# A decoder layer on one NeuronCore: the local-attention branch product as seven quarter products, GpSimd's additions on VectorE, and tables that fix places and orders

## The chip, the cores and the metric

The kernel runs on one core of one Trainium2 chip. The metric is the device time of one execution in microseconds (us); lower is better. A core has TensorE (PE in the profile; its weight loads are PEld), VectorE (DVE), ScalarE (ACT), GpSimd (POOL) and SyncE (SP), which here only issues transfers. Each engine works through its own instructions in a fixed order; semaphores make one wait for another. All arithmetic that decides the time is in float32, with TensorE reading a rounded format (`fp32r`).

## The reference, cut to what matters

One layer on x of 512 tokens by 1024, with three token mixers side by side, gates, an output projection and a gated feed-forward block:

```python
u = rms_norm(h, ln_mix_pre[l])
proj = jnp.einsum('bsd,de->bse', u, w_in[l])
qa, ka, va, qb, kb, vb, qm, gl = jnp.split(proj, split_idx, axis=-1)
y_swa = swa_sink_attention(...)         # local attention, 8 heads of 64, window 128
y_sb = stick_breaking_attention(...)    # 8 heads of 64
mkv = jnp.einsum('bmd,de->bme', rms_norm(mem, ln_mem[l]), w_mem_kv[l])
y_mem = memory_cross_attention(...)     # 4 heads of 128 on 256 memory rows
g = jax.nn.sigmoid(gl.reshape(B, S, N_BRANCH, D))
merged = (g[:, :, 0] * jnp.einsum('bse,ed->bsd', y_swa, w_branch_swa[l])
          + g[:, :, 1] * jnp.einsum('bse,ed->bsd', y_sb, w_branch_sb[l])
          + g[:, :, 2] * jnp.einsum('bse,ed->bsd', y_mem, w_branch_mem[l]))
mix = jnp.einsum('bsd,de->bse', merged, w_out[l])
h = h + rms_norm(mix, ln_mix_post[l])
u = rms_norm(h, ln_ffn_pre[l])
a = jax.nn.silu(jnp.einsum('bsd,df->bsf', u, w_gate[l])) * jnp.einsum('bsd,df->bsf', u, w_up[l])
h = h + rms_norm(jnp.einsum('bsf,fd->bsd', a, w_down[l]), ln_ffn_post[l])
```

The part that changes is `einsum(y_swa, w_branch_swa)`: 512 tokens by 512, times 512 by 1024.

## The kernel before, in words

**Three matmuls for one product.** Each operand x is split into a high part, x rounded to `fp32r` on ScalarE (line 137), and a low part, x minus the high part, on VectorE (line 138). A product is then three matmuls (`mm3`, lines 169 to 171): high by high, high by low, low by high.

**The stream of weights.** Weights come in pieces of 128 x 1024 (512 KB). `Stream` (line 34) holds a list of units. Each has a load (up to four units ahead), a split (up to three units ahead) and a generator of matmuls that yields its estimated time after each small group. `dn.run(us)` lets the stream issue that much work; between such calls the program issues the attention heads. So the code interleaves heavy products with attention, head by head. Four buffers each hold raw weights, high parts and low parts (`w_load`, `w_split`, lines 146 and 152).

**The order of the work.** The stream's units are, after the projections: the stick-breaking branch product, the gates of that branch, the gates of local attention, the product of local attention, the gates and the product of the memory branch. The memory heads (`mem_pair`, line 983) are issued in two pairs while the stream runs the local-attention product. One pair computes scores (`ms`), the softmax (`mw`: maxima, exponentials, scalings on line 1006), transposes (`mpt`, line 1012) and outputs (`ym`). The tile framework sorts what is issued into an order for each engine by its own estimates and by priorities; `after(...)` pins a few orders by hand.

**Seven products already in use.** The gates (`quart`, line 562) and the feed-forward block are computed with seven products of quarters in place of eight. Names p1 to p7 stand for these products. Their weights are sums of quarters, made by accumulating transfers on GpSimd's queue: `q_issue` (line 437) adds the next quarter from memory to a raw buffer that has been split (line 446). PSUM results are copied by ScalarE (line 540) or joined by VectorE.

**The branch product** (`branch_t`, line 577) is done plainly: for each half of the columns and each of four token tiles, four blocks of 128 by `mm3`, into one PSUM bank. VectorE multiplies the result by the gate (line 599). The addition to the sum of the branches (line 602) is GpSimd's, apart from the last token tile of the memory branch.

**Other work of GpSimd**: the sums of squares of the memory norm (lines 232 and 390), a low part of the position bias (line 810), scalings of the norms' gains (line 1058).

**Buffers.** 73 blocks of 128 x 512 (`ck`), 16 small ones, two PSUM pools of two and six banks (`dps`, `aps`). The weight pools are closed at the end of the mixers and their space is opened as the feed-forward's pool with nine raw buffers.

Of the kernel before, what the change touches and what calls it, by code (L numbers as in the profile page):

```python
# [29 lines left out]
QM_FIRST = 3  # L30
WARM = 10

# [74 lines left out]
def tile_kernel(ctx, tc, a):  # L107
    nc = tc.nc
# [4 lines left out]
    psd = ctx.enter_context(tc.tile_pool(name="psd", bufs=2, space=bass.MemoryType.PSUM))  # L113
    psa = ctx.enter_context(tc.tile_pool(name="psa", bufs=6, space=bass.MemoryType.PSUM))
    drm = ctx.enter_context(tc.tile_pool(name="drm", bufs=1, space=bass.MemoryType.DRAM))

    first = ExitStack()
    wp = first.enter_context(tc.tile_pool(name="wp", bufs=4))
    cst = first.enter_context(tc.tile_pool(name="cst", bufs=1))

    def ck(name, dt=F32):
        return ckp.tile([P, 512], dt, tag="ck", name=name)

    def small(name, n=4):
        return sm.tile([P, 8], F32, tag="s", name=name)[:, :n]

    def dps(name):
        return psd.tile([P, 512], F32, tag="d", name=name)

    def aps(name):  # L130
        return psa.tile([P, 512], F32, tag="a", name=name)
# [14 lines left out]
    def w_load(src, n):  # L146
        uid[0] += 1
        raw = wp.tile([P, 1024], F32, tag="raw", name=f"raw{uid[0]}")
        nc.sync.dma_start(raw[:, :n], src)
        return raw  # L150

    def w_split(raw, n):
        uid[0] += 1
        hi = wp.tile([P, 1024], F32R, tag="hi", name=f"hi{uid[0]}", bufs=4)
        lo = wp.tile([P, 1024], F32R, tag="lo", name=f"lo{uid[0]}", bufs=4)
# [32 lines left out]
    def after(ins, first):  # L188
        dep = mybir.DependencyInfo(mybir.DependencyClass.NoSync, mybir.DependencyReason.DATA)
        tc.add_manual_dep(ins.ins, first.ins.name, dep, reason="order")  # L190
# [18 lines left out]
    def const(name, shape, pool=cst):  # L209
        t = pool.tile(shape, F32, name=f"c_{name}")  # L210
        nc.sync.dma_start(t[:, :], a[name])
        return t
# [3 lines left out]
    ones = cst.tile([P, P], F32, name="ones")  # L216
# [11 lines left out]
    def rstd_of(name, acc, n, bank):  # L228


        if acc.shape[1] > n:
            nc.gpsimd.tensor_tensor(acc[:, :n], acc[:, :n], acc[:, n : 2 * n], op=ALU.add)
        ps = bank(f"ss_{name}")
        mm(ps[:, :n], ones[:, :], acc[:, :n], True, True)
        rb = cst.tile([P, n], F32, name=f"rb_{name}")
# [5 lines left out]
        rs = cst.tile([P, n // P], F32, name=f"rs_{name}")  # L241
# [102 lines left out]
    v_all = cst.tile([P, NT * 640], F32, name="v_all")  # L344
# [32 lines left out]
    def mem_split():  # L377
        acc = None
        for i, x in enumerate(st.pop("memT")):
# [9 lines left out]
            else:  # L389
                nc.gpsimd.tensor_tensor(acc[:, :], acc[:, :], x[:, :], op=ALU.add)  # L390
# [185 lines left out]

    def branch_t(b, h, q):


        def gen(hi, lo):  # L580
# [3 lines left out]
            for t in range(NT):  # L584
# [15 lines left out]
                eng = nc.vector if (b, t) == (MEM, NT - 1) else nc.gpsimd  # L600
# [27 lines left out]
    def add_proj(kind, idx, ci):  # L628
        dn.add(a["w_p"][:, ci].rearrange("p k n -> p (k n)"), 1024, proj(kind, idx))

# [24 lines left out]
    for b in (SB, SWA, MEM):  # L655
# [36 lines left out]
        if b != SB:  # L692
# [3 lines left out]
    xg = cst.tile([P, 544], F32, name="xg")  # L696
    g_pre, g_mem = xg[:, S : S + KC], xg[:, S + KC : S + 2 * KC]
    g_neg = cst.tile([P, KC], F32, name="g_neg")
# [20 lines left out]
    raws = [wp.tile([P, 1024], F32, tag="raw", name=f"raw_first{i}") for i in range(FIRST)]  # L719
    his = [wp.tile([P, 1024], F32R, tag="hi", name=f"hi_first{i}", bufs=4) for i in range(FIRST)]  # L720
    los = [wp.tile([P, 1024], F32R, tag="lo", name=f"lo_first{i}", bufs=4) for i in range(FIRST)]
# [10 lines left out]
    with tc.manual_schedule():  # L732

        idle = cst.tile([P, 512], BF16, name="idle")
# [48 lines left out]
    sinks = cst.tile([P, 8], F32, name="sinks")  # L783
# [3 lines left out]
    identb = cst.tile([P, P], BF16, name="identb")  # L787
    nc.gpsimd.tensor_copy(identb[:, :], ident[:, :])
    negm = cst.tile([P, P], BF16, name="negmb")
# [5 lines left out]
    def band_bias():  # L795
# [14 lines left out]
        nc.gpsimd.tensor_tensor(rbl[:32, :P], rb16[:32, :P], rbh[:32, :P].bitcast(F32), op=ALU.subtract)  # L810
# [25 lines left out]
    def pair_out(b, c, ps):  # L836

        y[(b, c)] = parts(f"y{b}{c}", ps)

# [293 lines left out]
    fac = {r: [(ck(f"{r}h{c}", F32R), ck(f"{r}l{c}", F32R)) for c in range(2)] for r in RIGHT}  # L1133
# [27 lines left out]
    def turn(t, tmp):  # L1161
# [5 lines left out]
        if t < 2:  # L1167
            turned[t] = [ck(f"ur{t}{h}") for h in range(2)]
            for h in range(2):
                place(("B11", "B21")[h], t, pt[h])  # L1170
                nc.scalar.copy(turned[t][h][:, :], pt[h][:, :])
# [4 lines left out]
        return place("T1", t, t1)  # L1176

# [21 lines left out]
    aq = {(i, j): [ck(f"aq{i}{j}{c}") for c in range(NCH)] for i in range(2) for j in range(2)}  # L1199
    sq = [ck(f"sq{c}") for c in range(NCH)]  # L1200
    sr = [ck(f"sr{c}") for c in range(NCH)]
# [16 lines left out]
    def g_raw(n, key, i, j):  # L1218
        uid[0] += 1
        gw[(n, key)] = fp.tile([P, 1024], F32, tag="raw", name=f"gw{uid[0]}")  # L1220
# [123 lines left out]
    ssd = [small(f"ssd{t}", 2) for t in range(NT)]  # L1344
# [8 lines left out]
    def dn_issue(p, c):  # L1353
# [3 lines left out]
        if p in ("p1", "p5", "p4"):  # L1357
            n = 512 * len(ks)
            src = a["w_dn"][:, h, j * HF + ks[0] : j * HF + ks[-1] + 1].rearrange("p k n -> p (k n)")
            if p == "p1":  # L1360
                rr[c] = fp.tile([P, 1024], F32, tag="raw", name=f"r{c}")
# [110 lines left out]
    first.close()  # L1472
    fp = ctx.enter_context(tc.tile_pool(name="fp", bufs=9, reuse_waits="tile"))

    def f_split(raw, n):
        uid[0] += 1
        hi = fp.tile([P, 1024], F32R, tag="hi", name=f"hi{uid[0]}", bufs=4)
        lo = fp.tile([P, 1024], F32R, tag="lo", name=f"lo{uid[0]}", bufs=4)
# [28 lines left out]
    load_at(4, g_raw, 0, "t", 1, 0)  # L1507
    load_at(4, g_plus, 0, "t", 0, 0)
# [34 lines left out]
    tmp[3] = mix(3)  # L1543
    turn(1, tmp[1])
    behind(since[-1], st["mixed"])
# [27 lines left out]
    go(len(fs.units))  # L1573

# [88 lines left out]
```

## Time and profile before

| | |
|---|---|
| runs | 787.07, 787.52, 788.17 us; median 787.52 |
| the profiled execution | 787.54 us |
| its span, first to last instruction | 785.7 us |
| granted TensorE clock, mean | 0.999 |
| PE busy | 776.3 us, 4638 matmuls |
| VectorE busy | 595.4 us |
| ScalarE busy | 469.3 us |
| GpSimd busy | 123.2 us |
| transfers | 128.61 MB |

The profile's times are counted from the start of the span; the device time is 1.84 us longer than the span. "PE busy" counts a matmul from its start to its modelled end, and consecutive matmuls overlap, so the distance from one start to the next tells the pace. "Idle before" is the time in which an engine did nothing ahead of an instruction, and the name behind the arrow is what ended it. The chain is followed back from the last instruction: at each step to what released it, or to the instruction before it on its engine.

### The profile page before, as it was taken

To read this page: it belongs to the slowest core of one execution; us is meant where nothing else is said; L and a number is where in the kernel's file an instruction comes from. 1 tells how busy PE (TensorE), PEld (TensorE's weight loads), DVE (VectorE), ACT (ScalarE), POOL (GpSimd) and SP (SyncE) were. 2 spreads that over 40 slices of the span, in tenths; PEclk is the share of its full clock that TensorE was granted. 3 is DMA by queue.
4 is the path that set the end of the run, shared out by engine and by line. 5 is a ranking of instruction groups with operands and counts; after the bars stand their busy time and mean duration, and the time that the engine had idled before them with its cause. 6 is when DMAs were issued, how large, how long until landed. Compare 5 with 4: busy or idle time off the path is not lost.

```text
span 785.7 us, 12335 instructions
## 1 busy us (share of the span) xinstructions
PE 776.3 (99%) x4638; PEld 682.2 (87%) x4638; DVE 595.4 (76%) x942; ACT 469.3 (60%) x837; POOL 123.2 (16%) x142
## 2 busy tenths in 40 slices
PE   9999999999999999999999999999999999999996
PEld 6899887788888888887888899999999999888885
DVE  6995876686877757876855599867677777898797
ACT  7663676686577666657633577455554455666673
POOL 0203400002011111321261000100000000215200
PEclk9999999999999999999999999999999999999999
DMA  8444923265449794369849418987666651949802
GB/s 301 132 138 121 314 88 108 81 190 124 89 100 206 178 208 139 54 170 250 304 162 255 92 47 219 260 220 191 186 180 183 186 155 54 222 107 239 184 1 108
DMA packets 44220, 128.61 MB, mean 164 GB/s; under 512 B 5248, under 2 KB 6832, under 8 KB 44160
## 3 DMA queue, kind: packets, MB, share of 16 engines
q1 hardware_dynamic: 30480, 85.21, 32.8%
q0 software_dynamic: 13248, 42.22, 27.8%
q8 instruction: 36, 0.59, 0.3%
q10 hardware_dynamic: 432, 0.39, 0.1%
q14 instruction: 24, 0.20, 0.1%
HBM read 120.98 MB, written 4.72 MB: 160 GB/s over the span
## 4 chain that ended last, share of the span: by engine, by line
PE 93%; DMA 2%; DVE 2%; issue 1%; ACT 1%; POOL 0%; DVEq 0%; SPq 0%; ACTq 0%; POOLq 0%
PE gx L169 5%; PE gx L171 5%; PE gx L170 5%; PE gy L171 3%; PE gy L169 3%; PE gy L170 3%; PE x L171 3%; PE x L170 3%; PE x L169 3%; PE br L169 2%; PE br L170 2%; PE br L171 2%; PE mx L171 2%; PE mx L170 2%; PE mx L169 2%; PE g1p L169 2%
## 5 line engine op out<-in xcount | busy, mean ns | idle before, releaser
L137 ACT CAST hi<-gw 128x1024 fp32r<-128x1024 f32 x77 | 79.9, 1048 | 92.7 <-DVE gw L1242 39.6
L138 DVE TENSOR_TENSOR lo<-raw,hi 128x1024 fp32r<-128x1024 f32 (+2 forms) x82 | 99.9, 1219 | 46.2 <-ACT hi L137 45.7
L138 DVE TENSOR_TENSOR lo<-gw,hi 128x1024 fp32r<-128x1024 f32 x77 | 93.5, 1223 | 36.2 <-ACT hi L137 36.2
L137 ACT CAST hi<-raw 128x1024 fp32r<-128x1024 f32 (+2 forms) x82 | 85.2, 1042 | 43.4 <-PE pv L171 13.0
L1224 POOL DMA_DIRECT2D gw<-in_w_gu x27 | 23.3, 883 | 196.4 <-DMA gw<-in_w_gu 91.3
L870 DVE TENSOR_TENSOR_SCAN bw<-br,bw 128x512 f32<-128x512 f32 (+3 forms) x32 | 24.4, 808 | 17.0 <-ACT bw L194 17.0
L137 ACT CAST hi<-r 128x1024 fp32r<-128x1024 f32 (+1 forms) x24 | 23.6, 982 | 19.8 <-PE y L171 5.3
L446 POOL DMA_DIRECT2D raw<-in_w_g x24 | 20.7, 862 | 93.2 <-DVE lo L138 74.2
L170 PE MATMUL x<-lo,lh 128*128 128x512 f32 x88 | 34.2, 389 | 0.0
L169 PE MATMUL x<-hi,lh 128*128 128x512 f32 x88 | 34.2, 389 | 0.0
L171 PE MATMUL x<-hi,ll 128*128 128x512 f32 x88 | 34.1, 389 | 0.0
L138 DVE TENSOR_TENSOR lo<-r,hi 128x1024 fp32r<-128x1024 f32 (+1 forms) x24 | 27.1, 1130 | 3.7 <-ACT hi L137 3.6
L137 ACT CAST hi<-bp 128x512 fp32r<-128x512 f32 x33 | 19.3, 620 | 13.4 <-PE y L171 4.8
L138 DVE TENSOR_TENSOR lo<-bp,hi 128x512 fp32r<-128x512 f32 x33 | 22.7, 721 | 6.0 <-ACT hi L137 5.8
L169 PE MATMUL gx<-B11h,hi 128*128 128x256 f32 x88 | 25.1, 285 | 0.2 <-ACT B11h L1153 0.2
L169 PE MATMUL gx<-T4h,hi 128*128 128x256 f32 x88 | 25.0, 285 | 0.0
L169 PE MATMUL gy<-N22h,hi 128*128 128x256 f32 x88 | 25.0, 284 | 0.0
L171 PE MATMUL gy<-N22h,lo 128*128 128x256 f32 x88 | 25.0, 284 | 0.0
L171 PE MATMUL gw<-B21h,lo 128*128 128x256 f32 x88 | 25.0, 284 | 0.0
L170 PE MATMUL gx<-B11l,hi 128*128 128x256 f32 x88 | 25.0, 284 | 0.0
L170 PE MATMUL gw<-B21l,hi 128*128 128x256 f32 x88 | 24.9, 283 | 0.0
L169 PE MATMUL gy<-T1h,hi 128*128 128x256 f32 x88 | 24.9, 283 | 0.0
(824 smaller groups left out, 2758.7 us busy)
## 6 DMA issues: line engine op xcount, KB each, us to landing
gw<-in_w_gu SPq DMA_DIRECT2D x57, 512.0 KB, 4.8
gw<-in_w_gu POOLq DMA_DIRECT2D x27, 512.0 KB, 7.5
raw<-in_w_g POOLq DMA_DIRECT2D x24, 512.0 KB, 6.0
raw<-in_w_g SPq DMA_DIRECT2D x18, 512.0 KB, 3.9
raw<-in_w_p SPq DMA_DIRECT2D x14, 512.0 KB, 4.5
raw<-in_w_brt SPq DMA_DIRECT2D x12, 512.0 KB, 4.8
bp<-in_w_dn SPq DMA_DIRECT2D x22, 256.0 KB, 10.3
r<-in_w_dn POOLq DMA_DIRECT2D x10, 512.0 KB, 9.1
```

The source lines that it names most:

```text
L137: ins = nc.scalar.copy(hi, raw)
L138: lows = nc.vector.tensor_tensor(lo, raw, hi.bitcast(F32), op=ALU.subtract)
L169: one = nc.tensor.matmul(out, lh, rh, start=start, stop=False, skip_group_check=True)
L170: nc.tensor.matmul(out, lh, rl, start=False, stop=False, skip_group_check=True)
L171: return one, nc.tensor.matmul(out, ll, rh, start=False, stop=stop, skip_group_check=True)
L446: nc.gpsimd.dma_start(t[:, :], src, accum_op=ALU.add)
L870: st["scan"] = nc.vector.tensor_tensor_scan(x, r, x, 0.0, op0=ALU.mult, op1=ALU.add)
L1224: nc.gpsimd.dma_start(gw[(n, key)][:, :], g_src(n, i, j), accum_op=ALU.add)
```

## The change

It has three parts.

1. **The product of local attention in seven quarter products** (`SEVENS = (SWA,)`). The tokens, the contraction and the columns are halved. `seven_raw` copies each head pair's output from PSUM, `seven_sums` forms four sums of quarters on VectorE, `seven_split` splits them, and the weights' sums come from accumulating transfers (`seven_issue`). Each of the seven units makes two pieces of 2 x 3 matmuls of 512 columns; p2 goes on in the bank of p1, p3 in that of p5, and p7 and p4 in that of p6, so the results of p1, p5, p6 and p7 are taken out in between (`seven_end`).
2. **GpSimd's additions on VectorE**: the gate sums of both branches, the sums of squares, the low part of the bias. The scalings of the gains go to ScalarE (`nc.scalar.mul`).
3. **Tables.** `PLAN` gives each tile its place by number, PSUM's eight banks become one pool, and constants, some raw buffers and the copies of p1 and p5 share one wide block. `ORDER` lists, for each engine, its calls by number in the order in which they stand in the code, and chains them in the listed order; `after` does nothing then. The feed-forward's pool is no longer opened behind a closed one. Two copies of transposed tokens (`kept`) and one load (unit 4 to 5) are issued later.

```diff
-                eng = nc.vector if (b, t) == (MEM, NT - 1) else nc.gpsimd
+                eng = nc.vector
...
-            nc.gpsimd.tensor_tensor(acc[:, :n], acc[:, :n], acc[:, n : 2 * n], op=ALU.add)
+            nc.vector.tensor_tensor(acc[:, :n], acc[:, :n], acc[:, n : 2 * n], op=ALU.add)
...
-            nc.gpsimd.tensor_scalar(t[h][:, :], t[h][:, :], -0.5, None, op0=ALU.mult)
+            nc.scalar.mul(t[h][:, :], t[h][:, :], -0.5)
...
+    def seven_issue(b, p):
+        j, h = QSRC[p]
+        src = a["w_brt"][:, b, h, 2 * j : 2 * j + 2].rearrange("p k n -> p (k n)")
+        if p in ("p1", "p2", "p3"):
+            sw[(b, p)] = w_load(src, 1024)
+            return
+        old = {"p5": "p1", "p6": "p5", "p4": "p6", "p7": "p3"}[p]
+        t = sw[(b, p)] = sw.pop((b, old))
+        nc.gpsimd.dma_start(t[:, :], src, accum_op=ALU.add)
...
+    def seven_sums(b):
+        a11, a12, a21, a22 = (yq.pop((b, j, i)) for i, j in ((0, 0), (0, 1), (1, 0), (1, 1)))
+        for out, x, y_, op in (
+            (a22, a21, a22, ALU.subtract),
+            (a21, a11, a21, ALU.subtract),
+            (a11, a22, a11, ALU.subtract),
+            (a12, a12, a11, ALU.add),
+        ):
+            nc.vector.tensor_tensor(out[:, :], x[:, :], y_[:, :], op=op)
...
+    def seven_end(b, p, i):
+        ps = sbank[i]
...
+        if p in ("p1", "p5"):
+            t = spare(f"s{p}{b}{i}")
+            with tc.high_priority():
+                nc.scalar.copy(t[:, :], ps[:, :])
+            skeep[(p, i)] = t
+        elif p == "p2":
+            seven_out(b, i, 0, ps)
+        elif p == "p3":
+            skeep[("y", i)] = join(ck(f"sy{b}{i}"), ps, skeep[("p1", i)], ALU.subtract)
+            z = skeep.pop(("p5", i))
+            nc.vector.tensor_tensor(z[:, :], z[:, :], skeep[("p1", i)][:, :], op=ALU.subtract)
+            skeep[("z", i)] = z
+        elif p == "p6":
+            t = skeep.pop(("y", i))
+            seven_out(b, i, 1, join(t, t, ps, ALU.subtract))
+        elif p == "p7":
+            t = skeep.pop(("z", i))
+            seven_out(b, 2 + i, 1, join(t, t, ps, ALU.subtract))
+        else:
+            t = skeep.pop(("p1", i))
+            seven_out(b, 2 + i, 0, join(t, ps, t, ALU.add))
...
+    def seven(b, p):
...
+        first, last = p in ("p1", "p5", "p6"), p in ("p2", "p3", "p4")
...
+        def gen(hi, lo):
+            for i in range(2):
+                if first:
+                    sbank[i] = (dps if p == "p5" else aps)(f"br{b}{p}{i}")
+                for k in range(2):
+                    mm3_behind(sbank[i][:, :], seven_left(b, p, k, i), cols((hi, lo), k * 512, 512), first and k == 0, last and k == 1)
+                yield 1.36
+                seven_end(b, p, i)
...
+    def add_sevens(b):
+        g0 = len(dn.units)
+        for p in QUART:
+            dn.add(seven_got(b, p), 1024, seven(b, p))
+        for g, p in enumerate(QUART):
+            if p not in ("p1", "p2", "p3"):
+                dn.units[g0 + g - 5]["begin"].append(lambda p=p: seven_issue(b, p))
+        dn.units[g0 - 4]["begin"].append(lambda: seven_sums(b))
+        for g, p in ((1, "p5"), (2, "p3"), (3, "p6"), (4, "p7")):
+            dn.units[g0 + g]["begin"].append(lambda p=p: seven_split(b, p))
...
+    for e, text in ORDER.items():
+        seen, last = getattr(nc, e).seen, None
+        for part in text.split():
+            a, _, b = part.partition("-")
+            for k in range(int(a), int(b or a) + 1):
+                if last is not None:
+                    follow(seen[k], seen[last])
+                last = k
```

From TensorE's table, the stretch of the product and of the gates behind it, and from SP's table the loads around it:

```diff
+        "1110-1331 1338 1332-1337 1339-1349 1374 1380 1350-1355 1362 1356-1361 1363-1373 1375-1379 1381-1482 1488 "
+        "1542-1547 1483-1487 1489-1529 1548-1550 1530 1536 1551-1556 1531-1535 1537-1541 1557-1591 1596-1597 "
+        "1592-1595 1598-1599 1610-1616 1600-1601 1617-1619 1636 1620 1624-1625 1621-1623 1637-1638 1626-1629 "
+        "1639-1647 1654-1655 1602-1609 1656-1659 1666-1668 1630 1669-1670 1631-1635 1648-1653 1660-1665 1671-1689 "
+        "1718-1723 1742 1704-1709 1690 1712 1710-1711 1691-1695 1713-1717 1743 1754 1744-1747 1755 1760 1756-1759 "
+        "1761-1765 1730-1732 1766 1772 1733-1735 1767 1696-1703 1768 1736-1737 1724 1738-1739 1725-1729 1740-1741 "
+        "1748-1753 1769-1771 1773-1826 1832 1827-1831 1833-1838 1844 1839-1843 1845-1855 1862 1856-1861 1863-1877 "
...
+        "0-14 16-18 15 19-27 32 28-31 33-34 36-38 35 39-52 57 60 53-56 63-64 58-59 61-62 65-90 93-94 91-92 97-98 "
+        "95-96 99-211"
```

Of the numbers in TensorE's table, 1542 to 1565 are the scores of heads 0 and 1, 1566 to 1601 the products p1, p2 and p5, 1602 to 1617 the transposes of heads 0 and 1, 1618 to 1629 p3, 1630 to 1641 the outputs of these heads, 1642 to 1665 the scores of heads 2 and 3, 1666 to 1695 p6, p7 and half of p4, 1696 to 1711 the transposes of heads 2 and 3, 1712 to 1717 the rest of p4, 1718 to 1723 the first of the memory branch's gates, 1724 to 1735 the outputs of heads 2 and 3, and from 1736 on the gates.

More of the change, by code (lines that the diff above doesn't have):

```diff
@@ L1176, in turn, with kept @@
         return place("T1", t, t1)
+    def kept(t):
+        turned[t] = [ck(f"ur{t}{h}") for h in range(2)]
+        for h in range(2):
+            nc.scalar.copy(turned[t][h][:, :], st[("kept", t)][h][:, :])
     def turn_n2(t):
@@ L1343, in tile_kernel @@
     gain_out = []
-    ssd = [small(f"ssd{t}", 2) for t in range(NT)]
+    ssd = Late(lambda t: small(f"ssd{t}", 2))
     held = []
```

234 lines of the change are left out of this document (192 added, 42 removed), and 98 rows, old and new, of tables (ORDER, PLAN).

## The prediction

> **What bounds the kernel now.** I read the page first, then the chain, then TensorE's timeline around the few places where it stands still. The page's engine line and the chain's shares by engine:
>
> ```profile
> PE 776.3 (99%) x4638; PEld 682.2 (87%) x4638; DVE 595.4 (76%) x942; ACT 469.3 (60%) x837; POOL 123.2 (16%) x142
> PE 93%; DMA 2%; DVE 2%; issue 1%; ACT 1%; POOL 0%; DVEq 0%; SPq 0%; ACTq 0%; POOLq 0%
> ```
>
> A busy PE is not by itself a PE at its peak, so the chain counts more: 93% of it is TensorE. The pace comes from TensorE's timeline of one undisturbed gate block (start, duration, line):
>
> ```profile
> 226.83 0.39 PE L171 MATMUL g1p<-hi,ul 128*128 128x512 f32 x1
> ...
> 264.46 0.39 PE L169 MATMUL g0p<-hi,uh 128*128 128x512 f32 x1
> ```
>
> From the first row to the second the program issues 166 matmuls of 512 columns: (264.46 - 226.83) / 166 = 0.2267 us each, though each lasts 0.39. TensorE loses time against this pace in few places; the two largest lie in the memory branch's gates, right behind the changed product:
>
> ```profile
> 355.24 0.39 PE L171 MATMUL g2p<-hi,xsp51l 128*128 128x512 f32 x1
> 356.60 0.50 PE L169 MATMUL g2p<-hi,xsp30h 128*128 128x512 f32 x1 [0.97 <-ACT gq2p L540]
> 356.94 0.40 PE L170 MATMUL g2p<-lo,xsp30h 128*128 128x512 f32 x1
> ...
> 372.82 0.39 PE L171 MATMUL g2p<-hi,ul 128*128 128x512 f32 x1
> 373.68 0.50 PE L169 MATMUL g2p<-hi,uh 128*128 128x512 f32 x1 [0.47 <-ACT gq2p L540]
> 374.02 0.40 PE L170 MATMUL g2p<-lo,uh 128*128 128x512 f32 x1
> ```
>
> Start to start, the first costs 356.60 - 355.24 - 0.23 = 1.13 and 0.11 more on the next matmul; the second 0.63 and 0.11. Together 1.98 us. The chain in order of time names the cause:
>
> ```profile
> 344.73 10.19 DMA raw<-in_w_g
> 355.01 0.67 ACT hi L137
> 355.97 0.59 ACT gq2p L540
> ...
> 365.13 5.29 DMA wo<-in_w_out
> 370.44 0.62 ACT wo12h L137
> 373.16 0.48 ACT gq2p L540
> ```
>
> Both times ScalarE's fixed order puts a rounding of a weight that has not landed ahead of the PSUM copy (gq2p) for which the next product waits. A transfer of 10.19 us, against a median of 6.0 (below), came later than the order allowed for.
>
> **The change part by part.** All sums are against the profiled execution: 787.54 us, span 785.7; the runs' median is 787.52, so one serves for the other.
>
> *The product.* The local-attention branch issues 8 outputs x 4 blocks x 3 = 96 matmuls of 512 columns; seven quarter products of 2 x 2 x 3 issue 84. That takes away 12 x 0.2267 = **2.72 us** on the path. The order table for TensorE has 4560 entries; before's 4638 matmuls are 4572 calls (66 in plain float run as two), so nothing else goes or comes there. [...]
>
> *What it adds on VectorE* (timelines of VectorE and GpSimd, and VectorE's rows by line):
>
> ```profile
> 326.15 1.13 DVE L1006 TENSOR_SCALAR mw<-mw,mden 128x256 f32<-128x256 f32 x4
> 332.38 0.67 DVE L138 TENSOR_TENSOR mpts20l<-mpt,mpts20h 128x512 fp32r<-128x512 f32 x1
> 332.97 0.67 DVE L138 TENSOR_TENSOR mpts21l<-mpt,mpts21h 128x512 fp32r<-128x512 f32 x1
> 329.13 2.72 DVE L1006 TENSOR_SCALAR mw<-mw,mden 128x256 f32<-128x256 f32 x4
> 329.32 1.58 POOL L602 TENSOR_TENSOR gq0p<-gq0p,bs 128x512 f32<-128x512 f32 x1
> L138 DVE TENSOR_TENSOR lo<-raw,hi 128x1024 fp32r<-128x1024 f32 (+2 forms) x82 | 99.9, 1219 | 46.2 <-ACT hi L137 45.7
> ```
>
> A 512-wide operation follows its like after 0.60 us (332.38, 332.97). The diff adds 4 sums of quarters, 4 low parts of them, 10 joins and, from GpSimd, 8 gate adds: 26 x 0.60 = 15.6 us. Three more weight splits (seven transfers for four) add 3 x 1.22 = 3.7. Back comes a stretch in which a GpSimd add held VectorE up: four scalings took 2.72 beside it and 1.13 without, 1.6 us. Net 15.6 + 3.7 - 1.6 = **+17.7 us**. Is there room?
>
> ```profile
> 280.00:300.00 20.00, 20.00 (x90) 16.57 (x89) 11.69 (x12) 12.60 (x17) 1.72 (x2) 1.00 0.86 213
> 300.00:320.00 20.00, 20.00 (x109) 17.25 (x109) 14.81 (x28) 12.30 (x28) 4.34 (x4) 1.00 0.25 81
> 320.00:340.00 20.00, 20.00 (x109) 17.16 (x108) 17.65 (x31) 11.60 (x27) 6.50 (x6) 1.00 0.37 74
> 340.00:360.00 20.00, 19.03 (x84) 15.43 (x84) 12.17 (x13) 12.44 (x18) 5.63 (x7) 1.00 0.87 213
> 360.00:380.00 20.00, 19.53 (x87) 15.80 (x86) 15.75 (x19) 15.57 (x23) 0.84 (x1) 1.00 0.98 302
> ```
>
> (Columns: length, then busy time of PE, weight loads, VectorE, ScalarE, GpSimd; clock; DMA share; GB/s.) In 300 to 340, where the product lies between the memory heads, VectorE is busy 14.81 + 17.65 = 32.5 us; with 17.7 that is 50.2 in 40 - 2.7 = 37.3: **12.9 us too much** if all stays there. Over 280 to 380 it is 72.1 + 17.7 = 89.8 in about 95.3: it fits, at 94%. What can move: the 4 sums and first splits forward into 280 to 300 (8.3 idle); the 8 gate adds (4.8 us) back, as nothing reads them until the memory branch; and the memory heads' own work, which only that branch reads. TensorE's table does the last: its run "1718-1723 1742 1704-1709 ... 1696-1703" sets transposes of heads 2 and 3 (1696 to 1711) behind products of the next gates (from 1718). A join waits for its product, and behind it on VectorE stand the low parts of the next weights, for which TensorE waits in turn. Between 0 and 12.9 us of such waits I take **0.6 us**, one wait of the size of the second above: the case lies near the end where neighbours and table make room. Both ends are kept for the range.
>
> *On ScalarE* the nearest rows by line:
>
> ```profile
> L194 ACT ACTIVATE sg<-gp 128x256 f32<-128x256 f32 x33 | 13.6, 413 | 2.8 <-DVE gp L1268 2.7
> L137 ACT CAST hi<-raw 128x1024 fp32r<-128x1024 f32 (+2 forms) x82 | 85.2, 1042 | 43.4 <-PE pv L171 13.0
> ```
>
> There come 8 copies of 256 columns when each head pair is done (by the nearest row, 413 ns, 3.3 us spread over 180 to 226), then 4 roundings and 4 copies of about 0.6 (0.62 and 0.59 in the chain above) and 3 roundings of a weight, 1.04: 7.9 us in 300 to 340, on 23.9. It fits; if not, a late copy of p1 or p5 holds the next product, as at 355. The bound is the rival's.
>
> *Transfers.* Four weight loads on SP become three there and four accumulating ones on GpSimd's queue. p1, p5, p6, p4 share a buffer, so each waits until VectorE has split the one before.
>
> ```profile
> 305.42 0.40 PE L169 MATMUL br<-hi,y00h 128*128 128x512 f32 x1
> ...
> 340.74 0.39 PE L170 MATMUL g2p<-lo,uh 128*128 128x512 f32 x1
> ```
>
> ```profile
> raw<-in_w_g POOLq DMA_DIRECT2D x24, 512.0 KB, 6.0
> DMA to landing us min/median/max: 5.1/6.0/10.2
> ```
>
> A step is landing, rounding, low part: 6.0 + 1.04 + 1.22 = 8.3 us, 12.5 at the longest; three steps 24.8 to 37.4. The old product runs from 305.4 to about 340 with the heads between; the new one is 2.7 shorter and p4 its last 2.7, so p4 starts some 29 us after p1, and p1's split may lie three units (3 x 12 x 0.2267 = 8.2 us) earlier: 37. By the median it fits with 12 us to spare, at the longest not quite, and I take the median because the DMA share there is 0.25 to 0.37: no wait. Behind these four on GpSimd's queue stand the next gates' transfers, which would be late with them.
>
> *Other moves.* The stretches with the cover:
>
> ```profile
> 60.00:80.00 20.00, 20.00 (x134) 19.42 (x133) 10.25 (x18) 6.08 (x7) 6.70 (x8) 1.00 0.43 130
> 380.00:400.00 20.00, 20.00 (x98) 16.82 (x97) 11.38 (x14) 8.03 (x13) 8.23 (x6) 1.00 0.47 175
> ```
>
> GpSimd's five adds ahead of the first attention heads go to VectorE, busy 10.25 of 20 in 60 to 80; six adds of the memory branch cost VectorE 3.6 us in 380 to 400, busy 11.38 of 20; four of six scalings of gains go to ScalarE near 400, busy 8.03 of 20 just ahead of it, two into the last product. Zero: each has idle time beside it. Without that cover it is 0.6 us an operation.
>
> *Tables.* Fixed places and orders add no work. They can win what TensorE loses: the 1.98 us, and small gaps such as this one at the first feed-forward product, which I don't count:
>
> ```profile
> 450.25 0.39 PE L169 MATMUL gx<-B11h,hi 128*128 128x256 f32 x1 [0.17 <-ACT B11h L1153]
> ```
>
> In SP's table 93-94 and 97-98, the memory branch's weights, now go ahead of 91-92 and 95-96, pieces of w_out; GpSimd's queue has no adds between its transfers; and TensorE's table often takes the first matmul of a next group ahead of the last of this one ("1826 1832 1827-1831"), which covers a late low part. I count the 1.98 as won, with 0 as the other end.
>
> Sum: 787.54 - 2.72 - 1.98 + 0.6 = **783.4 us**.
>
> **The rivals.**
> A, the forecast: 783.4, alone 781.8 to 784.5. Chance 0.42.
> B, only the matmuls go: the waits at 355 and 372 stay or are replaced by their like. For it: DMA share 0.87 and 0.98 there, and the six w_out loads keep their place in SP's table. 787.54 - 2.72 = 784.8, up to 786. Chance 0.27.
> C, VectorE becomes the bound between the memory heads. Place: joins of p6 and p7, which must empty their banks within one 1.36 us piece, queue behind splits and scalings. Price: of the 12.9 us, what doesn't move, with the old waits kept; with half, 787.54 - 2.72 + 6.4 = 791.2; with all, 797.7. Slower by more than 0.2% from 4.3 us of new waits on. For it: 17.65 of 20 already at 320. Against it: the table, and 5.5 us idle left over 280 to 380. Chance 0.21. [...]
> D, the accumulating transfers come late: 37.4 us for three steps against 29 if p1's split gets no lead, up to 8 us of waits; at half, on B's 784.8, 789. Chance 0.10.
>
> **How the numbers follow.** 0.2% (1.6 us) is about what a measurement can tell from no change: faster is below 785.9, slower above 789.1. A and most of B are faster, with a little of C and D: 0.70. Same: the rest of B, most of D, a little of C: 0.13. Slower: most of C, some of D: 0.17. The range reaches from 781.8 (A with no new wait, 782.8, less 1 us for small gaps) to 789.7, into C: about 0.17 is left out.
>
> **What would show it.** Right: 84 matmuls in the product; no gap over 0.5 us in TensorE's timeline from 300 to 375; VectorE near 90% there; last matmul near 775. B: gaps behind a copy of gq2p that waits for a transfer. C: gaps behind a VectorE join, with VectorE at 95% or more. D: ScalarE's rounding of a branch weight waiting for its DMA. What would make it wrong: a fixed order that holds one engine behind another anywhere else, which the change's text alone doesn't show.

## The result and the profile after

The change takes 783.84 us (median of six runs, 783.61 to 784.33), the kernel before 787.97 (six runs beside them, 787.07 to 789.26). The ratio is 0.9947, with a 95% interval of 0.9935 to 0.996: 4.1 us, or 0.5%, faster. The profiled execution took 783.61 us, its span 781.8.

In the changed kernel every instruction is recorded by one helper, so all have line 202, and PSUM's banks are all called p. Groups are told apart by their operands. The page's engine line, the chain's shares by engine, and what TensorE waited for:

```profile
PE 773.5 (99%) x4626; PEld 678.8 (87%) x4626; DVE 614.6 (79%) x982; ACT 480.7 (61%) x862; POOL 92.2 (12%) x121
PE 97%; DVE 1%; issue 0%; ACT 0%; DVEq 0%
```

```profile
PE p L202 <- DVE wide L202: 1.4, 1, 1.4
PE p L202 <- DVE lo L202: 0.6, 1, 0.6
```

Twelve matmuls fewer, and the chain is TensorE to 97% where it was 93%. The first wait is that for the first constant, which before has too; the second, 0.6 us, is the only one in the rest of the kernel that the view of waits lists. The stretch around the product, in the same columns as before:

```profile
300.00:320.00 20.00, 20.00 (x108) 16.52 (x107) 16.30 (x31) 16.89 (x37) 1.72 (x2) 1.00 0.62 132
320.00:340.00 20.00, 19.93 (x96) 15.51 (x95) 19.70 (x36) 12.61 (x28) 2.58 (x3) 1.00 0.64 134
340.00:360.00 20.00, 19.55 (x90) 15.62 (x88) 18.43 (x27) 15.21 (x22) 3.44 (x4) 1.00 0.96 232
360.00:380.00 20.00, 19.89 (x87) 16.28 (x88) 16.35 (x21) 14.56 (x21) 1.72 (x2) 1.00 0.93 265
```

VectorE is busy 36.0 us in 300 to 340, where it was 32.5: of the 17.7 us of new work that were forecast only 3.5 stay there. 340 to 380 went from 27.9 to 34.8.

Where the time came from is read off three marks in TensorE's timeline: the first matmul of the product (y00h), the first of the output projection (wo00h), and the last of all. Of after:

```profile
304.32 0.40 PE L202 MATMUL p<-hi,y00h 128*128 128x512 f32 x1
...
399.79 0.39 PE L202 MATMUL p<-wo00h,mgh 128*128 128x512 f32 x1
...
775.14 0.39 PE L202 MATMUL p<-hi,ll 128*128 128x512 f32 x1
```

Of before, where the first mark is at 305.42 (shown in the prediction):

```profile
402.82 0.39 PE L169 MATMUL mx<-wo00h,mgh 128*128 128x512 f32 x1
...
778.90 0.39 PE L171 MATMUL x<-hi,ll 128*128 128x512 f32 x1
```

Ahead of the product 1.10 us are won, between the first two marks ("the stage" below) 97.40 - 95.47 = 1.93, behind them 376.08 - 375.35 = 0.73. Some 0.4 of the 1.10 lie in the first 22 us, where executions differ: the matmul of the sums of squares starts at 22.21 in before and at 21.83 here, but at 21.91 and 22.84 in two kernels below that are the same as these up to there (before with the copies first, the change with two places altered). Both stages hold the same matmuls but for the 12 (456 and 444). So the stage lost 2.72 us of matmuls but became only 1.93 shorter: TensorE waits 0.8 us *more* there than before. The places at 355 and 372 are quiet, but this has come instead (TensorE, ScalarE, VectorE):

```profile
358.94 0.61 PE L202 MATMUL p<-hi,xsp60h 128*128 128x512 f32 x2
360.12 0.50 PE L202 MATMUL p<-lo,xsp60h 128*128 128x512 f32 x1 [0.56 <-DVE lo L202]
...
356.46 3.18 ACT L202 CAST hi<-raw 128x1024 fp32r<-128x1024 f32 x3 [1.66 <-issue]
...
357.71 2.35 DVE L202 TENSOR_TENSOR lo<-raw,hi 128x1024 fp32r<-128x1024 f32 x2
```

From 358.94 to 360.12 go two matmuls (0.45) and 0.73 of waiting, and 0.11 on the next. The rest is small: fifteen gaps of 0.08 to 0.21 between 312 and 345, 1.7 us together by TensorE's starts; eight of them, 1.05 us, lie in 320 to 340. What ends each of these the profile does not show.

### The profile page after: what moved, and what is told of

Its sections match the earlier page's. It is cut to its first block, busy times and chain, and to the rows that moved or that the text cites. A ratio compares the mean times of both kernels' runs of the same rounds, so it can differ in the third digit from the quotient of the medians.

```text
span 781.8 us, 12301 instructions
## 1 busy us (share of the span) xinstructions
PE 773.5 (99%) x4626; PEld 678.8 (87%) x4626; DVE 614.6 (79%) x982; ACT 480.7 (61%) x862; POOL 92.2 (12%) x121
## 4 chain that ended last, share of the span: by engine, by line
PE 97%; DVE 1%; issue 0%; ACT 0%; DVEq 0%
PE p L202 97%; DVE lo L202 0%; DVE gq0p L202 0%; DVE gq2p L202 0%; ACT hi L202 0%; DVE fg L202 0%; DVE wo03l L202 0%; DVEq L2035 0%; DVE wo11l L202 0%; DVE wo02l L202 0%; DVE s L202 0%; DVE wide L202 0%; DVE wo00l L202 0%; ACT sqr L202 0%; DVE wo01l L202 0%
## 5 line engine op out<-in xcount | busy, mean ns | idle before, releaser
L202 DVE TENSOR_TENSOR lo<-raw,hi 128x1024 fp32r<-128x1024 f32 (+4 forms) x138 | 157.9, 1152 | 53.4 <-ACT hi L202 52.8
L202 ACT CAST hi<-raw 128x1024 fp32r<-128x1024 f32 (+4 forms) x138 | 136.3, 997 | 86.5 <-PE p L202 49.5
L202 ACT CAST hi<-wide 128x1024 fp32r<-128x1024 f32 x57 | 59.7, 1052 | 38.8 <-PE p L202 15.6
L202 DVE TENSOR_TENSOR lo<-wide,hi 128x1024 fp32r<-128x1024 f32 x57 | 69.7, 1224 | 17.2 <-ACT hi L202 16.9
L202 PE MATMUL p<-lo,lh 128*128 128x512 f32 x154 | 59.9, 389 | 0.0
L202 PE MATMUL p<-hi,ll 128*128 128x512 f32 x154 | 59.7, 389 | 0.0
L202 PE MATMUL p<-hi,lh 128*128 128x512 f32 x154 | 59.1, 389 | 0.0
L202 PE MATMUL p<-lo,uh 128*128 128x512 f32 (+1 forms) x160 | 57.3, 358 | 0.0
L202 PE MATMUL p<-hi,ul 128*128 128x512 f32 (+1 forms) x160 | 57.2, 358 | 0.0
L202 PE MATMUL p<-hi,uh 128*128 128x512 f32 (+1 forms) x160 | 56.2, 359 | 0.0
```

What stands on the lines that cost most here:

```text
L202: ins = f(*args, **kw)
```

## The experiments

Times are medians, all against runs of before on the same chip (787.5 to 787.9). The stage and the rest are distances between the marks in each profiled execution.

| kernel | us | first mark | stage | rest |
|---|---|---|---|---|
| before | 787.97 | 305.42 | 97.40 | 376.08 |
| the change | 783.84 | 304.32 | 95.47 | 375.35 |
| no tables | 803.99 | 305.54 | 112.58 | 377.91 |
| additions only | 788.90 | 305.87 | 96.22 | 377.89 |
| seven products only | 801.07 | 305.20 | 109.51 | 377.81 |
| places only | 817.36 | 304.08 | 129.09 | 375.73 |
| TensorE's order and places | 843.98 | 307.00 | 134.47 | 390.80 |
| all orders but TensorE's | 789.68 | 300.19 | 105.40 | 375.57 |
| 12 matmuls more | 786.21 | 304.31 | 97.74 | 375.34 |
| gate additions on GpSimd | 786.90 | 304.55 | 99.65 | 375.35 |
| two places altered | 783.67 | 305.34 | 94.54 | 375.34 |
| the same and high parts first | 783.48 | 304.32 | 95.16 | 375.34 |
| before, copies first | 787.57 | 305.23 | 98.79 | 376.10 |
| four waits put in | 801.78 | 322.65 | 95.49 | 375.34 |

One row can't be read against the others as it stands: in the kernel with all orders but TensorE's, 24 matmuls of 512 columns come behind the first mark and not ahead of it (24 x 0.2267 = 5.4 us). Like for like its first mark is 305.6 and its stage 100.0.

### What the tables carry

The theory was that the 12 matmuls are worth 2.72 us anywhere and the tables gather about one more; the rival, that without the tables VectorE has no room. First the change without its tables:

```diff
-ORDER = { ... }
-PLAN = { ... }
+ORDER = {}
+PLAN = {}
```

> The change without its tables of places and orders: the framework sorts as it did before. Theory T1 (the 12 matmuls are worth 2.72 us anywhere, and the tables only gather about 1 us of small waits): 785.0 to 785.8, with the two waits of the memory branch's gates (1.13 and 0.63 us) still there. Rival T2 (the tables are what makes room on VectorE; without them the joins of the seven products queue behind splits and scalings): 789 to 795, with new waits of TensorE for VectorE between 300 and 345. Rival T3 (the tables alone carry the gain): 787.5 or more, with no new wait.

Measured: 803.99 us, ratio 1.0202 (1.0186 to 1.0218). The theory fell; the rival held, and worse than it said. The windows and the waits of TensorE:

```profile
300.00:320.00 20.00, 17.90 (x89) 14.41 (x87) 13.81 (x27) 12.51 (x28) 2.58 (x3) 0.91 0.64 123
320.00:340.00 20.00, 14.97 (x64) 12.34 (x64) 14.26 (x26) 11.17 (x27) 0.86 (x1) 0.81 0.29 73
340.00:360.00 20.00, 17.87 (x72) 13.89 (x71) 18.25 (x32) 8.69 (x14) 0.86 (x1) 0.85 0.34 80
```

```profile
PE mpt L51 <- DVE mw L51: 3.9, 2, 2.3
PE br0p L51 <- ACT sp L51: 3.2, 2, 2.8
PE ym L51 <- DVE mpts20l L51: 2.1, 1, 2.1
```

TensorE waits for VectorE's scalings (mw) and low parts and for ScalarE's copies (sp). VectorE is busy only some 14 of each 20 us in 300 to 340: it is not full, it does things in the wrong order. And the granted clock falls to 0.81, to which the last experiment returns.

Then the seven products alone, with all additions and scalings where they were before (five lines; one shown):

```diff
-        nc.vector.tensor_tensor(g[:, :], g[:, :], more[:, :], op=ALU.add)
+        nc.gpsimd.tensor_tensor(g[:, :], g[:, :], more[:, :], op=ALU.add)
```

> The seven products alone: GpSimd keeps its additions and scalings as before, no tables. T1: 785.0 to 785.8 as without tables, since neither the additions nor the tables carry the 2.72 us. T2: 2 to 4 us below the kernel without tables, because VectorE is relieved of ten additions of 0.6 us there; still above before. T4: 1 to 2 us above the kernel without tables, as a GpSimd addition beside four scalings doubles their time.

801.07 us, ratio 1.0164 (1.0148 to 1.0179): 2.9 us below the kernel without tables, inside T2's span. So the new product without an order for it costs 13 us, 12.1 of them in the stage. The places without the orders:

```diff
-ORDER = { ... }
+ORDER = {}
```

> The change with its table of places (and the copies of p1 and p5 in a place of their own, PSUM as one pool of eight) but without its table of orders. T1: within 0.5 us of the kernel without tables, as what TensorE loses is lost by order. Rival T5 (the buffers, PSUM banks above all, decide): within 0.5 us of the whole change, 783.4 to 784.4. A third way: places made for another order hold the framework's order back, 790 or more.

817.36 us, ratio 1.0368: the third way. That the places were made for another order is the likely reason; which of them holds what back was not looked into. Outside the stage, though, this kernel has nearly all that the change wins there: its first mark is 304.08, its rest 375.73. Last, TensorE's order alone, and all orders but TensorE's:

```diff
-ORDER = {"tensor": ..., "vector": ..., "scalar": ..., "gpsimd": ..., "sync": ...}
+ORDER = {"tensor": ...}
```

> The change with its places and with TensorE's table alone; the framework sorts the other four engines. If TensorE's order is what makes room (it puts the memory heads' transposes behind products of the next gates): 784 to 787, with under 3 us of waits between 300 and 380. If VectorE's and ScalarE's orders carry it as much: 792 or more, with waits of TensorE for VectorE's scalings and low parts as in the kernel without tables.

843.98 us, ratio 1.0711: far outside both. Its view of waits begins with 17.2 us for ScalarE's gq2p in two waits, which suggests that the framework sorts ScalarE's copies behind other work. This run is not a clean one: with any table present, the orders pinned by hand (`after`) are off too.

```diff
-ORDER = {"tensor": ..., "vector": ..., "scalar": ..., "gpsimd": ..., "sync": ...}
+ORDER = {"vector": ..., "scalar": ..., "gpsimd": ..., "sync": ...}
```

> The change with all its tables but TensorE's, which the framework sorts. If TensorE's order makes the room: 795 to 804, near the kernel without tables, with waits between 300 and 360. If the other engines' orders carry it: 784 to 786.

789.68 us, ratio 1.002 (1.001 to 1.0029), between the two: 14.3 of the 20.2 us that separate the kernel without tables from the change come back with the places and the other engines' orders, and 5.8 with TensorE's. These shares hold for this way of adding the tables up, with the pinned orders off here too: TensorE's order added to the places alone, in the run before, made the kernel 26.6 us slower. None does it alone.

### Is TensorE the bound in the changed product?

```diff
+                    for _ in range(2 if first and k == 0 else 0):
+                        nc.tensor.matmul(sbank[i][:, :], seven_left(b, p, k, i)[0], hi[:, :512], start=True, ...)
                     mm3_behind(sbank[i][:, :], ...)
```

(TensorE's table is renumbered, with each copy ahead of its original.)

> The change with 12 matmuls more: each first matmul of p1, p5 and p6 (six of them) is issued three times in a row into its bank, so the result stays. If TensorE bounds the product as it stands in the change: 12 x 0.2267 = 2.7 us more, 786.3 to 786.8, and the small waits there stay. If VectorE bounds it (busy 19.70 of 20 us in 320 to 340): the matmuls go into waits, at most 1.5 us more, under 785.4.

786.21 us, 2.37 more than the change and just under the first span; the stage grew by 2.27. TensorE is the bound: of 2.72 us only 0.45 went into small gaps, and the wait at 359 stayed at its size. This is also the price of what the change removed, measured in place.

### What the additions on VectorE are worth

On the kernel before's plain product, without tables:

```diff
-SEVENS = (SWA,)
+SEVENS = ()
-ORDER = { ... }
-PLAN = { ... }
+ORDER = {}
+PLAN = {}
```

> GpSimd's additions on VectorE and the gains' scalings on ScalarE alone: plain product, no tables. T1 (idle time hides them, and VectorE gets back what GpSimd's additions cost it): 787.1 to 787.7, no change. Rival T2 (VectorE is already short between the memory heads; eight gate adds of 0.6 us there delay the low parts): 788.5 to 791. Rival T4 (the contention of the two engines was worth time on the path): 785.5 to 786.5.

788.90 us, ratio 1.001 (1.0001 to 1.0018): the number of T2, by another way. The stage became 1.2 us *shorter*, and the wait at 355 is gone: the first accumulating transfer of that place, issued at 345.12, lands at 353.45, where before's landed at 354.92. The loss lies outside: the first feed-forward product waits 1.41 us for ScalarE's B11h (0.17 in before). The first mark is 0.45 later too, but that arose in the first 22 us, where executions differ.

```profile
450.84 0.39 PE L51 MATMUL gx<-B11h,hi 128*128 128x256 f32 x1 [1.41 <-ACT B11h L51]
```

The same wait of 1.41 stands in both other kernels without any table (rest 377.8 to 377.9). Now the reverse: the change in its own order, but the eight gate additions on GpSimd, entered in its table where their inputs are ready.

```diff
-        nc.vector.tensor_tensor(g[:, :], g[:, :], more[:, :], op=ALU.add)
+        nc.gpsimd.tensor_tensor(g[:, :], g[:, :], more[:, :], op=ALU.add)
```

> The change with the eight gate additions of the product back on GpSimd, everything else in the tables' order. If VectorE has room by the order (the prediction's step): within 0.4 us of the change, 783.4 to 784.3. If VectorE is the bound there: 783.0 or less, by up to 8 x 0.6 us for those that lie ahead of the wait at 359. If the additions on GpSimd hold VectorE up or GpSimd's transfers behind them: 784.5 to 786, with four scalings at 2.7 us in place of 1.1 and later landings at 353 to 361.

786.90 us, 3.1 more than the change (the profiled execution took 788.03; in it TensorE's pace fell behind the longer wait, to 0.43 us from 364.19 to 364.62, as in the last experiment). The timeline of GpSimd, VectorE and TensorE between 350 and 363:

```profile
352.43 2.87 POOL L206 TENSOR_TENSOR gq0p<-gq0p,bs 128x512 f32<-128x512 f32 x2
356.54 1.68 POOL L206 TENSOR_TENSOR gq0p<-gq0p,bs 128x512 f32<-128x512 f32 x1 [1.24 <-DVE gq0p L206]
...
352.69 3.17 DVE L206 TENSOR_TENSOR wo02l<-wo,wo02h 128x512 fp32r<-128x512 f32 x1
356.99 1.78 DVE L206 TENSOR_TENSOR wo03l<-wo,wo03h 128x512 fp32r<-128x512 f32 x1
...
359.94 0.61 PE L206 MATMUL p<-hi,xsp60h 128*128 128x512 f32 x2
362.90 0.50 PE L206 MATMUL p<-lo,xsp60h 128*128 128x512 f32 x1 [2.34 <-DVE lo L206]
```

The first of these low parts in the change:

```profile
351.69 0.68 DVE L202 TENSOR_TENSOR wo02l<-wo,wo02h 128x512 fp32r<-128x512 f32 x1
```

A low part that takes 0.68 us in the change took 3.17 beside two GpSimd additions and 1.78 beside one; the four scalings at 311 took 2.62 in place of 1.14. So the additions on GpSimd save VectorE nothing: over the whole run it is busy 615.1 us without these eight operations and 614.6 with them. The wait at 359 grew from 0.73 to 2.5 us, a new one of 0.83 came at 312, and the accumulating transfers hardly moved (last landing 361.04, in the change 360.99). The 3.17 us end at 355.86 and the 1.78 at 358.77, each some 0.55 us behind the end of a GpSimd addition (355.30 and 358.22). What holds VectorE up there the runs don't show.

What the additions are worth depends on the order, though. In the framework's order, without tables, the kernel with all of them on GpSimd was 2.9 us faster than the one with all on VectorE (801.07 and 803.99).

### The waits in the memory branch's gates

The prediction put before's two waits down to ScalarE's order. So in before that order alone was changed:

```diff
                 dn.add(q_got(b, p, c), 1024, quart(b, p, c))
+                if b == MEM and c == 1 and p in ("p5", "p7"):
+                    dn.units[-1]["split_ahead"] = 2
```

> The kernel before, with ScalarE's order changed at the two places of the prediction's first part: the roundings of late weights are split one unit later in p5 and p7 of the memory branch's gates, so that they stand behind the copies of gq2p. If that order is the cause of the two waits: 1.1 to 2.0 us less than before, 785.9 to 786.8, with no wait at 355 and 373 for the copy. If the late transfer is the cause: the product that needs the late weight waits as long a little later, within 0.4 us of before.

787.57 us, ratio 0.9996 (0.9987 to 1.0005): nothing. The copies at 355 come in time, but TensorE now waits later (timeline of the profiled execution, which took 788.73, the longest of the eleven):

```profile
367.98 0.50 PE L169 MATMUL g2p<-hi,uh 128*128 128x512 f32 x1 [1.70 <-ACT gq2p L540]
...
365.88 1.05 ACT L137 CAST hi<-raw 128x1024 fp32r<-128x1024 f32 x1 [0.92 <-DMA raw<-in_w_g]
366.83 0.61 ACT L137 CAST wo03h<-wo 128x512 fp32r<-128x512 f32 x1
367.35 1.06 ACT L540 COPY gq2p<-g2p 128x512 f32<-128x512 f32 x2
```

The same picture one product on: a rounding stood until 365.78 for its transfer, another rounding went ahead, and the copy came behind both. The order moved the wait. That no order would remove it is not shown, as here too a late rounding stands ahead of a copy; and in this execution the first transfer took 11.34 us where it took 10.19 in before's. The second place is no test: there the prediction's chain names the rounding of wo12h, the edit moved the rounding of a gate weight, and wo12h still stands ahead of the copy. TensorE still waits there, 0.60 us at 374 and 0.59 at 376 by its starts.

In the change, the order does decide. Its ScalarE table puts a rounding first whose buffer TensorE frees only at 356.4, ahead of the more urgent one, whose weight landed at 356.03:

```diff
 scalar: "... 405
-407 401
+401 407
 vector: "... 458
-464 460 430 462 461
+460 464 461 430 462
```

> The change with two places of its tables altered: ScalarE rounds the weight of the next product (its transfer landed at 356.03) ahead of one whose buffer TensorE frees only at 356.4, and VectorE takes the low parts of the next two products ahead of that one's and of a gate addition. If the wait at 359 (0.72 and 0.11 us) comes from this order: it goes, 782.9 to 783.2, and the low part is ready at about 358.9 for a matmul at 359.17. If the accumulating transfers beside w_out are what is late, whatever the order: no change, 783.7 to 784.2, or the wait moves to the next product.

783.67 us, above the span given. But the wait is gone (four rows where it stood, in this kernel 1 us later because its first matmuls of all ran at the lower pace for longer in this execution, 0.43 us apart from 6.08 to 6.94, where the change's come 0.23 apart from 5.60 on):

```profile
359.67 0.39 PE L205 MATMUL p<-hi,xsp31l 128*128 128x512 f32 x1
359.89 0.61 PE L205 MATMUL p<-hi,xsp60h 128*128 128x512 f32 x2
360.35 0.39 PE L205 MATMUL p<-lo,xsp60h 128*128 128x512 f32 x1
360.57 0.39 PE L205 MATMUL p<-hi,xsp60l 128*128 128x512 f32 x1
```

The stage is 0.93 us shorter than the change's; in the medians 0.17 us remain, which can't be told from none. With TensorE taking high parts first as well, in p6 (and its table to match, both token tiles' high parts ahead of the low ones):

```diff
+                    for k in range(2):
+                        for x in q_left(p, c, k, i):
+                            nc.tensor.matmul(qbank[key][:, :], x, hi[:, k * 512 : (k + 1) * 512], ...)
+                    for k in range(2):
+                        nc.tensor.matmul(qbank[key][:, :], q_left(p, c, k, i)[0], lo[:, k * 512 : (k + 1) * 512], ...)
```

> As the run with two altered places, and TensorE issues in p6 of the memory branch's gates all matmuls that need only the weights' high part ahead of those that need the low part (8 of 12, 1.8 us of cover in each of two units). The order of a sum changes, the result only by rounding. If low parts are late there by less than 1.8 us: 782.9 to 783.2, no wait over 0.1 us from 355 to 375; it can't be told from the run with the two places alone if that run has none left. If a transfer is late: the wait shows in front of the high part instead, 783.6 or more.

783.48 us, the stage 0.6 us longer than with the two places alone:

```profile
364.10 1.07 ACT L206 COPY gq2p<-p 128x512 f32<-128x512 f32 x2 [2.67 <-PE p L206]
...
364.74 0.50 PE L206 MATMUL p<-hi,uh 128*128 128x512 f32 x1 [0.22 <-ACT gq2p L206]
```

It made a wait of its own: with the low parts of both token tiles last, the first tile's bank is done later, its copy too, and the next product starts on that bank. Neither is shown to beat the change.

### What a wait costs beyond itself

The kernels without tables were slower than their waits. Four waits were therefore put where TensorE runs undisturbed: ScalarE repeats a copy on which the next product waits.

```diff
+AGAIN = {(SB, "p5", 0): 4, (SB, "p6", 0): 6, (SWA, "p5", 0): 5, (SWA, "p6", 0): 7}
...
             st["chain"] = nc.scalar.copy(t[:, :], ps[:, :])
+            for _ in range(AGAIN.get((b, p, i), 0)):
+                nc.scalar.copy(t[:, :], ps[:, :])
```

> The change with four waits of TensorE put into the first two gate blocks, where it runs undisturbed: ScalarE repeats the copy of p5 or p6 of the first token tile 4, 6, 5 and 7 times (0.47 us each; the next product on that bank waits for the last one, after some 0.6 us of cover): about 1.3 us near 242, 2.2 near 253, 1.75 near 280, 2.7 near 292. If a wait costs itself alone: 8.0 us more in all, 791.5 to 792.3, and matmuls go on at 0.227 us behind each. If, as the rows of the kernels without the tables of orders suggest, a wait of over some 2.1 us is followed by matmuls at 0.427: the second and the fourth cost 2 to 3 us more each, 795 to 798, the first and the third do not.

801.78 us (799.03 to 804.15), 17.9 more than the change. The waits were longer than sized, 1.95, 3.18, 2.56 and 4.03 us start to start, 11.7 in all; 6.2 are left. Behind the shortest and behind the next:

```profile
241.39 0.39 PE L206 MATMUL p<-hi,xsp51l 128*128 128x512 f32 x1
243.56 0.50 PE L206 MATMUL p<-hi,xsp30h 128*128 128x512 f32 x1 [1.79 <-ACT gq1p L206]
243.90 0.40 PE L206 MATMUL p<-lo,xsp30h 128*128 128x512 f32 x1
...
287.69 0.39 PE L206 MATMUL p<-hi,xsp51l 128*128 128x512 f32 x1
290.49 0.50 PE L206 MATMUL p<-hi,xsp30h 128*128 128x512 f32 x1 [2.40 <-ACT gq0p L206]
...
291.05 0.60 PE L206 MATMUL p<-hi,xsp30l 128*128 128x512 f32 x1
291.45 0.63 PE L206 MATMUL p<-hi,xsp30h 128*128 128x512 f32 x1
...
294.43 0.42 PE L206 MATMUL p<-lo,xsp30h 128*128 128x512 f32 x1
294.70 0.40 PE L206 MATMUL p<-hi,xsp30l 128*128 128x512 f32 x1
```

After 1.79 us of standing still TensorE goes on at its pace; after 2.40 it issues eight matmuls from 291.05 to 294.43, 0.42 us apart: 1.6 us lost on top. The waits that came out over 2.1 us, three of the four, all cost so, the first did not; the total lies above the span given because they came out longer. The windows show the same as a lower granted clock (the column behind the engines), here behind the first wait and behind the second, of 3.18 us:

```profile
244.00:248.00 4.00, 4.00 (x19) 3.18 (x18) 2.69 (x3) 2.95 (x4) 1.42 (x2) 1.00 0.49 81
260.00:264.00 4.00, 4.00 (x11) 3.09 (x11) 1.86 (x3) 0.96 (x2) 0.00 (x0) 0.53 0.46 131
```

## Why the prediction came out right, step by step

**The sum.** 783.4 was forecast, 783.84 measured. That they agree so well is partly luck: the waits came out 2.2 us worse than forecast (0.8 more in place of 1.4 fewer), and 1.8 us that the prediction had set to nothing made up for it. Of its signs three came: 84 matmuls, VectorE at 88% (70.8 of 80 us from 300 to 380), the last matmul at 775.14. One did not: at 359 TensorE stood for 0.56 us, where no gap over 0.5 was to be.

**The product, 2.72 us.** Right in mechanism: twelve extra matmuls in the changed product cost 2.37.

**"I count the 1.98 as won", and 0.6 for new waits.** This is where the sum went wrong. The two named waits did go, but the stage shows 2.72 - 1.93 = 0.8 us more waiting than before, so new waits took 1.98 + 0.8 = 2.8 us, not 0.6: 0.8 of them at 359, most of the rest in gaps of 0.1 to 0.2. VectorE is busy 19.70 of 20 us where the larger part of these lies; that it causes them is likely but not shown. For this stage that is what rival B said, the waits replaced by their like, with a touch of C. What made the sum come out is a term that the prediction named and set to nothing, the small gaps: 1.10 us ahead of the product (some 0.4 of it perhaps this execution's) and 0.73 behind the stage. In the kernel without tables neither is won (first mark 305.54, rest 377.91); with the table of places alone nearly all of both is (304.08 and 375.73). So they come with the places, and what comes with them: PSUM as one pool, and no feed-forward pool behind a closed one. These were not tried apart.

**The cause of the two waits** was given as ScalarE's order, which puts a late weight ahead of the copy. Changed alone, in before, at the first place, that order won nothing: the wait moved to 366. At the second place it was not tested. In the kernel with the additions alone the transfer landed 1.5 us earlier and the wait at 355 went. It was not issued earlier there (345.12 and 344.73) but took 8.3 us in place of 10.2. As it took 11.3 in the run with the copies first, executions may differ by as much; whether the additions have to do with it stays open.

**VectorE: 17.7 us more, 12.9 too much, covered by the table.** Right in kind, but the load was over-sized. Over the whole run VectorE is busy 19.2 us more (595.4 and 614.6); the prediction's prices give 17.7 and, at 0.6 each, 6.6 for the eleven other additions. Without the tables the stage is 15.2 us longer than before and the listed waits alone come to 9.2 us; with them the one at 359 and the small gaps are left. Of the moves that were to make room, the prediction gave the memory heads' to TensorE's table; added last, that table brings the smaller part, 5.8 us of 20.2. **The 1.6 us that GpSimd's contention was to give back** was too small: in the kernel with the additions alone 19 operations more, 11.4 us at 0.6 each, raised VectorE's busy time by only 2.9 (595.4 and 598.3). In the tables' order the eight additions are worth 3.1 us of device time, since the delayed low parts lie ahead of a wait of TensorE.

**ScalarE fits** as to its load, but one order in its table made the wait at 359. **The accumulating transfers of the product** fit, as forecast: p5, p6, p7 and p4 took 5.6 to 7.7 us and TensorE waited for none, so rival D did not come. **The other moves at nothing** holds in the tables' order. In the framework's, the kernel with the additions alone lost 1.8 us behind the stage; but so did the one with the seven products alone (1.7), which has none of these moves. What both have and before has not is the third part's later copies and load, and tiles that are made only when first used; these were not tried alone.

**Rival C** was priced at 797.7 with nothing moved. The kernel that shows it took 804.0 (801.1 with the additions on GpSimd). The price lacked the lower clock, 0.91, 0.81 and 0.85 in its three windows above: in the stage of that kernel's profiled execution 33 matmuls come 0.38 to 0.59 us apart, some 7 us more than at 0.2267.

## What to carry to other kernels

A saving on the bound engine is worth its price only if the other engines can deliver in that order: here the same kernel, 12 matmuls shorter, took 16 us more than before or 4 less, by orders and places alone. When a stage's wait is named by a profile, ask whether its place is set by the order or by a transfer: changing the order at one place, while the transfers were late, only moved the wait. And price a wait of TensorE at more than its length where it comes near those that cost more here: behind a stand of 2.40 us matmuls came 0.42 us apart and 1.6 us went on top, behind one of 1.79 nothing did.

## What the runs showed of the hardware

**TensorE's pace fell to about half behind seven stands of 2.11 to 3.02 us.** The granted clock was near 0.5 behind the one of 3.02 (0.53 from 260 to 264 in the windows above). In the kernel with the seven products alone a stand of 2.11 us, with two of 1.45 and 0.77 in the four us ahead of it, was followed by ten matmuls 0.427 us apart (timeline of TensorE):

```profile
338.63 0.80 PE L51 MATMUL br0p<-hi,ys0p7h 128*128 128x512 f32 x1 [2.11 <-ACT ys0p7h L51]
339.22 0.63 PE L51 MATMUL br0p<-lo,ys0p7h 128*128 128x512 f32 x1
339.65 0.63 PE L51 MATMUL br0p<-hi,ys0p7l 128*128 128x512 f32 x1
```

Single stands of 1.64, 1.78 and 1.79 us in three places were not followed so; the seven from 2.11 to 3.02 us were, for 2.5 to 5.7 us. The length of one stand alone doesn't decide it here. With TensorE's order alone, two stands of 0.97 and 0.77 us with one matmul between them were enough, and one of 3.49 was followed by four matmuls at full pace and only after a second stand by slow ones:

```profile
365.79 0.49 PE L133 MATMUL p<-hi,xsp50h 128*128 128x512 f32 x1 [0.97 <-ACT hi L133]
367.05 0.50 PE L133 MATMUL p<-lo,xsp50h 128*128 128x512 f32 x1 [0.77 <-DVE lo L133]
367.38 0.43 PE L133 MATMUL p<-hi,xsp50l 128*128 128x512 f32 x1
367.62 0.63 PE L133 MATMUL p<-hi,xsp50h 128*128 128x512 f32 x1
368.04 0.63 PE L133 MATMUL p<-lo,xsp50h 128*128 128x512 f32 x1
```

The slow matmuls came 0.427 us apart, against 0.2267 in the undisturbed block. 2.40 us of standing still in one piece (in the kernel with the four waits), or 1.74 in two (with TensorE's order alone), came ahead of them. What decides was not measured.

**A VectorE operation beside GpSimd additions** took 3.17 us (352.69 in the kernel with the gate additions on GpSimd) in place of 0.68 (351.69 in the change), as shown above.
